# A hybrid decoder step: the 32x32 inverses of the delta net on one compact tile that ScalarE fills and empties

## Chip, cores and metric

The kernel runs on one core of a Trainium2 chip. The metric is the time of one execution on the device in microseconds (us), as the median of several runs. TensorE is called PE here, VectorE DVE, ScalarE ACT, GpSimd POOL, and SyncE, which issues the DMAs, SP.

## The reference

Two decoder layers run over a prompt of 512 tokens and 8 sequences of 8 new tokens, 576 tokens in all, of width 1024. Layer 0 has a pooling mixer, layer 1 a gated delta net, and each is followed by a SwiGLU FFN of width 2816. All is float32. The change is in the delta net, which the reference computes in chunks of 64 tokens (the kernel takes 128):

```python
kb = k * beta[..., None]
a_mat = jnp.where(strict, jnp.einsum('bhnid,bhnjd->bhnij', kb, k) * decay, 0.0)
t_mat = a_mat + jnp.eye(CHUNK, dtype=jnp.float32)
solve = functools.partial(lax.linalg.triangular_solve, left_side=True, lower=True, unit_diagonal=True)
u = solve(t_mat, v * beta[..., None])
w = solve(t_mat, kb * jnp.exp(gc)[..., None])
...
def step(S, inp):
    u_i, w_i, qk_i, qd_i, kd_i, gl_i = inp
    v_new = u_i - jnp.einsum('bhck,bhkv->bhcv', w_i, S)
    o_i = jnp.einsum('bhck,bhkv->bhcv', qd_i, S) + jnp.einsum('bhcs,bhsv->bhcv', qk_i, v_new)
    S = S * gl_i[..., None, None] + jnp.einsum('bhck,bhcv->bhkv', kd_i, v_new)
    return S, o_i
```

The unit triangular matrix of each head and chunk has to be inverted. 16 heads by 4 chunks of 128 tokens make 64 matrices of 128x128.

## The kernel before

**Work.** Large products are made of three passes with operands split into a high and a low part (`wh`, `wl` of the weights; `hH`, `hL` of the activations). `Weights.load` brings a weight block by DMA (`wraw`), ACT writes `wh`, and DVE or POOL subtracts to give `wl`. The stages follow each other: layer 0 with its FFN, the delta net in four groups G of four heads, its output projection, and the FFN of layer 1.

**A group.** `project(G)` computes q, k, v of the group (PSUM tile `ps_m`, two banks in turn; ACT moves them out to `u`, DVE convolves them in `ac`). `core(G)` is the delta rule: DVE writes the 16 triangular matrices of the group into `Uw` (128 partitions, 16 matrices, 128 columns), `inv32` inverts the four 32x32 diagonal blocks of all 16, and products on PE (`ps_k`, `ps_s`, with ACT between them in `Rs`, `T01`, `R2`) merge the blocks to 128x128. `braid` writes `inv32` down together with `sample_front`, the same step for the sample group, and `scan` with `sample_heads` follows.

**inv32.** `A` (tile `ia`) receives the transposed blocks, each column twice, and `X` (the first half of tile `ii`) begins as the identity `eye2`. For m from 31 down to 1, DVE multiplies into a scratch `tv` (the second half of `ii`) and subtracts from X: 62 small instructions. Before that, one DVE transpose for each of the four partition blocks reads `Uw` directly (`ia<-Uw`), and after it one for each writes back (`Uw<-ii`). The next user of the blocks is `T01` (`T<-Uw`, DVE), and then PE.

**Order.** Nothing is issued as it is written. All calls are recorded by `Plan`, with their dependences on tiles and banks, and `finish` places them on the five engines by ranks and costs (`forward`). Instructions that are marked EITHER go to DVE or POOL. Where a gap of PE in the plan is long, `idle_until` fills it with matmuls on an unused bank (`ps_w<-ones`). Last, `refined` goes through the program in windows and stirs the ranks by the seeds in the table `CHOSEN`, so another table gives another order everywhere. All recorded instructions therefore carry line 531, where they are issued, and the fillers line 527.

Of the kernel before, what the change touches and what calls it, by code (L numbers as in the profile page):

```python
# [14 lines left out]
AF = mybir.ActivationFunctionType  # L15
# [5 lines left out]
P = 128  # L21
# [35 lines left out]
class Plan:  # L57
# [755 lines left out]
def hybrid_kernel(  # L813
# [593 lines left out]
    def inv32(ap_, W):  # L1407
# [5 lines left out]
        for b in range(4):  # L1413
            s = slice(32 * b, 32 * b + 32)
            DVE.transpose(A[s], W[s, :, 32 * b:32 * b + 32].rearrange("p h i -> p i h").unsqueeze(2)
                          .to_broadcast([32, 32, 2, 16]))
            yield 1.2
# [817 lines left out]
```

## Time and profile before

| | |
|---|---|
| median of 3 runs | 1526.5 us (1526.38 to 1527.4) |
| the profiled execution's own time | 1525.06 us |
| its span, from the first to the last instruction | 1523.3 us |
| granted PE clock, mean | 0.997 |
| instructions | 30379 |

Rows of a group give: line, engine, operation, tile written and tiles read, shapes, count, then busy us in all, mean ns of one, and the engine's idle time before them with what ended it. Names of tiles leave buffer numbers out (`T` is `T01`). PEld is PE's loading of weights, which overlaps its matmuls. A float32 matmul shows as two records, so a filler counts twice in the trace and once in the order.

### The profile page before, as it was taken

The page shows a single profiled execution, that of the slowest core. Times are in us where ns is not written, and L with a number is a line of the kernel's source. Part 1 is how long each engine was busy: PE and PEld are TensorE (multiplying, and loading weights), DVE is VectorE, ACT ScalarE, POOL GpSimd, SP SyncE. Part 2 cuts the span into 40 slices and gives each one's busy share as a digit, 9 for nine tenths or more (in the row PEclk, how much of TensorE's full clock was granted, in tenths as well). Part 3 has the DMA queues.
Part 4 walks back from the last instruction along what each step waited for, and adds up shares of the span by engine and source line. Part 5 has one row for each costly group of instructions (what it writes and reads, how often), then busy time and mean ns, then how long its engine had stood idle before and what let it go on. Part 6 is the DMA issues. An engine that isn't in the chain of part 4 may idle for free.

```text
span 1523.3 us, 30379 instructions
## 1 busy us (share of the span) xinstructions
PE 1501.0 (99%) x11850; PEld 1452.8 (95%) x11850; DVE 1155.7 (76%) x2284; ACT 840.6 (55%) x1815; POOL 129.4 (8%) x269
## 2 busy tenths in 40 slices
PE   8999999999999999999999999999999999999997
PEld 7999999999999899899899899999999999999997
DVE  6993566678688698997899799667896476766865
ACT  7753543435466975764763764545565453534553
POOL 4210000000011010121120120100110000000000
PEclk9999999999999999999999999999999999999999
DMA  6563323233457433335433544657765333233263
GB/s 190 156 188 110 98 74 111 67 99 104 148 170 204 114 88 111 102 103 147 111 112 93 147 127 128 202 158 220 240 184 155 109 87 96 83 89 110 66 196 99
DMA packets 344902, 197.86 MB, mean 130 GB/s; under 512 B 13547, under 2 KB 337740, under 8 KB 344751
## 3 DMA queue, kind: packets, MB, share of 16 engines
q1 hardware_dynamic: 344759, 195.92, 44.6%
q8 instruction: 93, 1.52, 0.4%
q14 instruction: 50, 0.41, 0.1%
HBM read 165.60 MB, written 30.52 MB: 129 GB/s over the span
## 4 chain that ended last, share of the span: by engine, by line
PE 88%; DVE 6%; ACT 3%; DMA 2%; issue 1%; POOL 0%; SPq 0%; DVEq 0%; ACTq 0%; POOLq 0%
PE ps_B L531 29%; PE ps_A L531 26%; PE ps_m L531 19%; PE ps_s L531 5%; PE ps_k L531 5%; PE ps_x L531 2%; PE ps_e L531 1%; DVE wl L531 1%; PE ps_n L531 1%; DVE Uw L531 1%; DMA vt<-z_d 1%; DVE ac L531 1%; ACT wh L531 1%; DMA wraw<-in_gdn_w_in_dram 0%; DMA yo<-y_d 0%
## 5 line engine op out<-in xcount | busy, mean ns | idle before, releaser
L531 ACT ACTIVATE wh<-wraw 128x1024 fp32r<-128x1024 f32 (+4 forms) x239 | 232.5, 978 | 201.5 <-PE ps_B L531 79.6
L531 DVE TENSOR_TENSOR wl<-wraw,wh 128x1024 fp32r<-128x1024 f32 (+4 forms) x231 | 258.3, 1122 | 76.0 <-ACT wh L531 40.3
L531 PE MATMUL ps_m<-hH,wh 128*128 128x320 f32 (+1 forms) x832 | 251.5, 313 | 0.0
L531 PE MATMUL ps_m<-hL,wh 128*128 128x320 f32 (+1 forms) x832 | 247.5, 306 | 0.1
L531 PE MATMUL ps_m<-hH,wl 128*128 128x256 f32 (+1 forms) x832 | 245.8, 308 | 0.1
L531 PEld LDWEIGHTS ps_m<-hH,wh 128*128 128x128 f32 x832 | 155.1, 190 | 4.0 <-issue 1.0
L531 PEld LDWEIGHTS ps_m<-hL,wh 128*128 128x128 f32 x832 | 156.0, 190 | 2.0 <-issue 0.8
L531 PEld LDWEIGHTS ps_m<-hH,wl 128*128 128x128 f32 x832 | 154.7, 190 | 1.7 <-issue 0.4
L531 PE MATMUL ps_B<-hH,wh 128*128 128x320 f32 (+1 forms) x444 | 127.8, 304 | 0.2
L531 PE MATMUL ps_B<-hL,wh 128*128 128x320 f32 (+1 forms) x444 | 127.1, 304 | 0.0
L531 PE MATMUL ps_B<-hH,wl 128*128 128x320 f32 (+1 forms) x444 | 127.1, 304 | 0.0
L531 PE MATMUL ps_A<-hH,wh 128*128 128x256 f32 (+1 forms) x432 | 119.4, 292 | 0.0
L531 PE MATMUL ps_A<-hL,wh 128*128 128x256 f32 (+1 forms) x432 | 117.7, 290 | 0.0
L531 PE MATMUL ps_A<-hH,wl 128*128 128x256 f32 (+1 forms) x432 | 117.5, 291 | 0.1
L531 PE MATMUL ps_B<-aL,wh 128*128 128x288 f32 x352 | 100.0, 296 | 0.0
L531 PE MATMUL ps_B<-aH,wl 128*128 128x288 f32 x352 | 99.2, 297 | 0.7 <-DVE wl L531 0.7
L531 PE MATMUL ps_B<-aH,wh 128*128 128x288 f32 x352 | 99.1, 298 | 0.5 <-DVE xa L531 0.5
L531 PE MATMUL ps_A<-aL,wh 128*128 128x288 f32 x352 | 98.3, 296 | 0.0
L531 PE MATMUL ps_A<-aH,wl 128*128 128x288 f32 x352 | 97.7, 297 | 0.0
L531 PE MATMUL ps_A<-aH,wh 128*128 128x288 f32 x352 | 97.1, 297 | 0.0
L531 PEld LDWEIGHTS ps_B<-hH,wh 128*128 128x128 f32 x444 | 81.7, 188 | 0.7 <-ACT wh L531 0.6
L531 DVE SCALAR_TENSOR_TENSOR ac<-u,cwt,ac 128x600 f32<-128x600 f32 x96 | 79.5, 837 | 3.3 <-ACT ac L531 3.1
(463 smaller groups left out, 4040.8 us busy)
## 6 DMA issues: line engine op xcount, KB each, us to landing
wraw<-in_ffn_w_in_dram SPq DMA_DIRECT2D x77, 512.0 KB
wraw<-in_gdn_w_in_dram SPq DMA_DIRECT2D x56, 512.0 KB
graw<-in_ffn_w_in_dram SPq DMA_DIRECT2D x33, 512.0 KB
wraw<-in_ffn_w_out_dram SPq DMA_DIRECT2D x32, 448.0 KB
wraw<-in_gdn_w_out_dram SPq DMA_DIRECT2D x24, 512.0 KB
wraw<-in_ffn_w_out_dram SPq DMA_DIRECT2D x32, 320.0 KB
St<-in_state_gdn_rec_dram SPq DMA_DIRECT2D x32, 256.0 KB
out_dram<-St SPq DMA_DIRECT2D x32, 256.0 KB
```

The costliest lines, as they stand in the source:

```text
L531: calls[e](*a, **k)
```

## The change

`inv32` gathers the four diagonal blocks of `Uw` into the second half of `ii` with four ACT copies, each 32 partitions by 512. One DVE transpose over all 128 partitions then fills `A`. At the end one DVE transpose over 128 partitions writes the result into the second half of `ii`, and four ACT copies spread it back into `Uw`. The recursion between is untouched. The table `CHOSEN` is another one: 5 strings with 3206 numbers in the place of 6 with 3493. So the order of instructions differs through the whole program, and which of the EITHER instructions go to POOL too.

```diff
     CHOSEN = (
-        "0: 51633 4180 93590 78750 34477 23530 63076 77272 88530 16072 91213 50029 90818 92607 6488 48788 652 "
...
         A = ap_.tile([P, 32, 32], F32, name="ia", tag="ia", bufs=1)
         XT = ap_.tile([P, 2, 512], F32, name="ii", tag="ii", bufs=1)
         X = XT[:, 0].rearrange("p (j i) -> p j i", j=32)
+        D32 = XT[:, 1].rearrange("p (i h) -> p i h", h=16)
         for b in range(4):
             s = slice(32 * b, 32 * b + 32)
-            DVE.transpose(A[s], W[s, :, 32 * b:32 * b + 32].rearrange("p h i -> p i h").unsqueeze(2)
-                          .to_broadcast([32, 32, 2, 16]))
-            yield 1.2
+            ACT.activation(D32[s], W[s, :, s].rearrange("p h i -> p i h"), AF.Copy)
+        DVE.transpose(A, D32.unsqueeze(2).to_broadcast([P, 32, 2, 16]))
+        yield 1.2
         EITHER.tensor_copy(X, eye2)
...
+        DVE.transpose(XT[:, 1].rearrange("p (i j) -> p i j", j=32), X.rearrange("p j i -> p i j"))
         for b in range(4):
             s = slice(32 * b, 32 * b + 32)
-            DVE.transpose(W[s, :, 32 * b:32 * b + 32].rearrange("p h (i d) -> p i d h", d=2),
-                          X[s].rearrange("p j i -> p i j"))
+            ACT.activation(W[s, :, s].rearrange("p h i -> p i h"), D32[s], AF.Copy)
             yield 0.6
```

**The start of an inverse, third group (G = 2).** These are DVE's rows before, from the last matrices in `Uw` to the first step of the recursion; `des` belongs to the sample group and `ac` to the convolutions of the next group.

```order
1083 L531 SCALAR_TENSOR_TENSOR Uw<-ps_k,bet,QD 128x128 x2
1084 L531 RECIPROCAL oss<-oss 128x20
1085 L531 STREAM_TRANSPOSE ia<-Uw 32x1024 x4
1086 L531 TENSOR_TENSOR des<-des,s_st 128x128
1087 L531 TENSOR_TENSOR ii<-ia,ii 128x31
1088 L531 SCALAR_TENSOR_TENSOR ac<-u,cwt,ac 128x600
```

The same place on DVE in the changed kernel, where `BD` and `TQ` belong to the sample group:

```order
1071 L514 SCALAR_TENSOR_TENSOR Uw<-ps_k,bet,QD 128x128
1072 L514 TENSOR_TENSOR des<-des,s_in 128x128
1073 L514 TENSOR_TENSOR QD<-ps_k,QD 128x2x128 x2
1074 L514 TENSOR_TENSOR wl<-wraw,wh 128x1024
1075 L514 SCALAR_TENSOR_TENSOR BD<-ps_k,bet,des 64x64 x2
1076 L514 TENSOR_TENSOR TQ<-ps_k,des 64x64 x2
1077 L514 STREAM_TRANSPOSE ia<-ii 128x1024
1078 L514 SCALAR_TENSOR_TENSOR BD<-ps_k,bet,des 64x64
1079 L514 TENSOR_TENSOR ii<-ia,ii 128x31
```

And ACT there in the changed kernel, with the gather among the moves out of `ps_m`:

```order
728 L514 ACTIVATE QD<-QD,ngs 128x128
729 L514 ACTIVATE wh<-wraw 128x1024
730 L514 ACTIVATE ii<-Uw 32x512 x4
731 L514 ACTIVATE u<-ps_m 128x256
732 L514 ACTIVATE ks<-ps_k 128x128
733 L514 ACTIVATE u<-ps_m 128x8x8
```

One transpose stands in the place of four, a weight split and steps of the sample group moved ahead of it, and the four copies stand on ACT directly ahead of a move out of `ps_m`.

**The end of an inverse, first group (G = 0).** DVE before, from the last step of the recursion to the third transpose into `T01`:

```order
754 L531 TENSOR_TENSOR ii<-ii 128x16
755 L531 STREAM_TRANSPOSE Uw<-ii 32x32x16 x2
756 L531 STREAM_TRANSPOSE T_1431<-Uw 32x16x32 x2
757 L531 STREAM_TRANSPOSE Uw<-ii 32x32x16 x2
758 L531 SCALAR_TENSOR_TENSOR ac<-u,cwt,ac 128x600
759 L531 TENSOR_TENSOR wl<-wraw,wh 128x1024
```

DVE in the changed kernel:

```order
748 L514 TENSOR_TENSOR ii<-ii 128x16
749 L514 STREAM_TRANSPOSE ii<-ii 128x512
750 L514 TENSOR_TENSOR wl<-wraw,wh 128x1024
751 L514 STREAM_TRANSPOSE T_1431<-Uw 32x16x32 x2
752 L514 TENSOR_TENSOR wl<-wraw,wh 128x1024
753 L514 STREAM_TRANSPOSE T_1431<-Uw 32x16x32
```

ACT in the changed kernel, where `zz` is a gate projection that is moved out of `ps_m`:

```order
513 L514 ACTIVATE u<-ps_m 128x256
514 L514 ACTIVATE Uw<-ii 32x32x16 x4
515 L514 ACTIVATE wh<-wraw 128x1024
516 L514 ACTIVATE zz<-ps_m 128x256
517 L514 ACTIVATE Rs_1432<-ps_k 32x16x32 x2
```

The four transposes back became one transpose and four copies on ACT, and a weight split fills DVE's wait for the copies.

**PE at the start of the third group's inverse.** Before, with the fillers `ps_w` around the first products of the sample group (`qks`):

```order
4614 L531 MATMUL ps_s<-gts,s_gt_r 128x256
4615 L531 MATMUL ps_k<-qk 128x256
4616 L527 MATMUL ps_w<-ones 128x128
4617 L531 MATMUL ps_k<-qks 128x128
4618 L531 MATMUL ps_k<-ident,qks 128x128
4619 L527 MATMUL ps_w<-ones 128x128 x4
4620 L531 MATMUL ps_m<-hH,wh 128x256
```

In the changed kernel the first product of the sample group stands among projections, with no filler near:

```order
4647 L514 MATMUL ps_m<-hH,wh 128x320
4648 L514 MATMUL ps_m<-hL,wh 128x320
4649 L514 MATMUL ps_k<-qks 128x128
4650 L514 MATMUL ps_m<-hH,wl 128x320
4651 L514 MATMUL ps_m<-hH,wh 128x320
4652 L514 MATMUL ps_k<-ident,qks 128x128
```

Counted over the whole order, there are 42 fillers before and 36 now: 8 and 9 at the start, 6 and 6 at the change from layer 0 to layer 1, 18 and 9 in the four groups of the delta net, 10 and 12 at the end. The eight `wl` splits that POOL made before are on DVE now. ACT has 31 table loads where it had 30.

384 rows, old and new, of the table CHOSEN are left out of this document.

## The prediction

> **What bounds the kernel now.** I read the page first, then the table of stretches, the groups by form, and the chain of waits inside the delta net. The page's first part, busy time by engine, its DVE row by slices, and its chain:
>
> ```profile
> PE 1501.0 (99%) x11850; PEld 1452.8 (95%) x11850; DVE 1155.7 (76%) x2284; ACT 840.6 (55%) x1815; POOL 129.4 (8%) x269
> DVE  6993566678688698997899799667896476766865
> PE 88%; DVE 6%; ACT 3%; DMA 2%; issue 1%; POOL 0%; SPq 0%; DVEq 0%; ACTq 0%; POOLq 0%
> ```
>
> PE is the bound: it is idle for 1523.3 - 1501.0 = 22.3 us, and every matmul of the reference is still there after the change. What can change is how well PE is fed. The table of stretches tells where it isn't; after the stretch and its length come busy us of PE, PEld, DVE, ACT and POOL, then clock and DMA.
>
> ```profile
> 0.00:38.00 38.00, 32.34 (x219) 29.78 (x220) 25.08 (x72) 28.97 (x70) 17.81 (x77) 0.91 0.69 190
> 440.00:520.00 80.00, 78.30 (x629) 73.75 (x628) 65.42 (x136) 56.99 (x131) 8.08 (x17) 1.00 0.61 168
> 520.00:975.00 455.00, 449.96 (x3921) 420.10 (x3920) 400.46 (x963) 287.31 (x808) 75.29 (x144) 1.00 0.43 123
> 1100.00:1460.00 360.00, 359.94 (x2718) 359.02 (x2718) 252.39 (x408) 173.55 (x270) 5.10 (x6) 1.00 0.39 114
> 1460.00:1523.00 63.00, 53.69 (x402) 50.93 (x400) 36.53 (x63) 30.89 (x57) 0.00 (x0) 0.97 0.47 140
> ```
>
> The four groups of the delta net are 520 to 975 us. DVE is busy for 400.46 of 455 us there (88%), against 70% in the last FFN. PE shows 5.04 us of idle time, and PEld is busy for 92.3%, against 99.7% in the FFN. So DVE is nearly full where the change relieves it, but PE's own row leaves little to win. Start and end hold 5.66 and 9.31 us of idle PE, which this code doesn't touch.
>
> The Trainium skill, in "Perfetto Trace Analysis", Identifying the Most-Contended Engine, says that matmul busy time is a poor measure of headroom and that the busy share of weight loads is a good one. By it the stage would have 34.9 us to give where the matmul row has 5.04. The FFN's row agrees with the rule, but the stage also loads many narrow weights, so I take it as a ceiling.
>
> **The change part by part.** The groups by form, with busy us and mean ns of one:
>
> ```profile
> L531 DVE STREAM_TRANSPOSE ia<-Uw 32x1024 f32<-32x1024 f32 x16 | 32.6, 2034 | 0.2
> L531 DVE STREAM_TRANSPOSE Uw<-ii 32x512 f32<-32x512 f32 x16 | 18.2, 1138 | 0.4
> L531 DVE STREAM_TRANSPOSE T<-Uw 32x512 f32<-32x512 f32 x12 | 8.4, 701 | 0.3
> L531 ACT ACTIVATE s1h<-s1raw 128x512 fp32r<-128x512 f32 x33 | 20.8, 629 | 26.9 <-DVE s1raw L531 12.5 <-PE ps_A L531 8.0 <-PE ps_B L531 6.3
> L531 DVE COPY ii<-eye 128x512 f32<-128x512 f32 x3 | 1.3, 417 | 0.0
> L531 POOL TENSOR_TENSOR wl<-wraw,wh 128x1024 fp32r<-128x1024 f32 x8 | 19.3, 2414 | 18.5 <-ACT wh L531 18.5
> L531 DVE TENSOR_TENSOR wl<-wraw,wh 128x1024 fp32r<-128x1024 f32 x151 | 184.4, 1225 | 39.4 <-ACT wh L531 22.9 <-PE ps_B L531 7.8 <-PE ps_A L531 7.2
> L531 ACT ACTIVATE u<-ps_m 128x256 f32<-128x256 f32 x56 | 20.7, 375 | 19.1 <-PE ps_m L531 18.6 <-PE ps_x L531 0.3
> L531 ACT ACT_TABLE_LOAD x29 | 37.2, 1283 | 1.1 <-DMA misc<-in_gdn_a_log_dram 0.7
> L527 PE MATMUL ps_w<-ones 128*128 128x128 f32 x84 | 14.4, 300 | 1.3 <-POOL ones L306 1.3
> ```
>
> *DVE's load.* Removed: 32.6 + 18.2 = 50.8 us. Added: four transposes of 1024 and four of 512, now over 128 partitions. The trace has none over 128. A transposed element takes 701 / 512 = 1.37 ns where source and target run densely (`T<-Uw`), and 2.0 to 2.2 ns in the two removed forms. So the 1024 costs 1.40 to 2.03 us, and I take 1.40, since its source is dense now. The 512 costs 0.70 to 1.14 us, and I take 1.14, since its source still strides. Together that is 10.2 us (8.4 to 12.7), and DVE is relieved by 40.6 us. The eight splits that come over from POOL cost DVE 8 x 1.225 = 9.8 us of it. That leaves about 31 us, and DVE's share of the stage falls from 88% to 81%. On its own this is worth nothing in time, since PE is the bound.
>
> *ACT's load.* 32 copies of 512 at 0.629 us make 20.1 us. No ACT row of this size has a strided operand; strides make DVE's transposes 1.45 to 1.6 times as long, so the bounds are 20 to 32 us, and I take 20, as the copies read or write densely on one side. ACT has 455 - 287.31 = 167.7 us free in the stage, which hides it. One more table load is 1.28 us of ACT, hidden as well (0 to 1.3).
>
> The Trainium skill speaks against these copies: "ScalarE: Activation LUTs", Rules for kernel authors, wants simple elementwise work on VectorE and not on ScalarE. The one copy of 512 on DVE agrees, with 0.417 us against 0.629. By that rule the 32 copies would be 13.3 us on DVE and the relief 27 us in place of 40.6; with ACT's free time in the stage I follow the load and not the rule.
>
> *The end of an inverse.* The chain of waits inside the first group's end, then the fourth's (start us, us, what):
>
> ```profile
> 585.82 1.13 DVE Uw L531
> 586.98 1.17 DVE Uw L531
> 588.17 0.70 DVE T L531
> 588.88 0.70 DVE T L531
> 589.60 0.88 DVE Uw L531
> 590.78 1.14 DVE Uw L531
> ...
> 950.88 1.07 DVE Uw L531
> 951.99 1.16 DVE Uw L531
> ...
> 955.78 1.14 DVE Uw L531
> ```
>
> The transposes back lie on the chain in these two groups; in the second and third the chain runs elsewhere. From 585.82 to 591.92 they take 6.10 us. After the change, one transpose of 1.14, then four copies of 0.629 one behind the other, 3.66 us, with both `T` transposes on DVE beside the copies. So 2.4 us less in each of the two, 4.9 us on the chain. But DVE and PE wait on each other all along here, and PE is busy beside it: shortening the chain helps only where PE would else run dry. I can bound this from 0 to -4.9 us, and take the middle, -2.4.
>
> *The start of an inverse.* DVE is held for 8.09 us in one piece now (the timeline of DVE, then of ACT, in the third group):
>
> ```profile
> 779.64 8.09 DVE L531 STREAM_TRANSPOSE ia<-Uw 32x1024 f32<-32x1024 f32 x4
> 785.24 0.50 ACT L531 ACTIVATE u<-ps_m 128x256 f32<-128x256 f32 x2 [3.12 <-PE ps_m L531]
> ```
>
> After: four copies, 2.5 us, and 1.40 us of transpose, about 4 us shorter. None of these four pieces is on the chain, so I take 0 for the latency (bounds 0 to -4 us a group). The waits that it adds: the transpose waits for ACT's copies, and behind it stands the recursion; in the third group a split of 1.2 us and steps of the sample group stand ahead of it and cover half of the copies. If that cover is gone, the recursion starts up to 2.5 us later, still earlier than now. The copies also need `ii` free of the states that were stored from it, which only the identity copy needed so early before.
>
> *The fillers.* PE is given fillers where the plan leaves it a gap, so their count tells of gaps. 84 records in 14.4 us are 42 fillers of 0.34 us. The stage has 18 now and 9 after: -3.1 us. Start and end have 3 more: +1.0 us. Net -2.1 us (0, if the gaps are only left empty, to -3.1).
>
> *Sum.* 0 (loads) - 2.4 (ends of inverses) - 2.1 (gaps) = -4.5 us. Against the profiled execution, 1525.06 us (the span of 1523.3 and 1.8 around it), that is 1520.6. Its own time lies 1.4 us under the median of the runs, so on the median 1526.5 - 4.5 = 1522.0 us.
>
> **The rivals.** *No change.* PE shows no idle time that DVE could fill: 449.96 of 455 us. Then what leaves DVE's chain turns up as PE's own, fillers only hid gaps that other waits keep, and the time is 1526.5 to 1525, say 1525.5. For it: 88% of the chain is PE already. Against it: half the fillers of the stage are gone.
>
> *More than forecast.* If the weight loads' row is the true headroom, the end of every inverse counts in full: 4 x 2.4 + 2.1 = 11.7 us, 1514.8. For it: 92.3% against 99.7%. Against it: in two groups the chain passes elsewhere.
>
> *Slower: the copies hold up the moves out of `ps_m`.* ACT works in order, and at the eight places the four copies stand as a block of 2.5 us directly ahead of, or close to, `u<-ps_m` or `zz<-ps_m`. The projections have two banks. How fast PE fills one, from a long run of them in the chain:
>
> ```profile
> 780.72 12.80 PE ps_m L531 x96
> ```
>
> And a weight split's copy on ACT, from its timeline:
>
> ```profile
> 787.04 1.06 ACT L531 ACTIVATE wh<-wraw 128x1024 fp32r<-128x1024 f32 x1 [1.29 <-PE ps_m L531]
> ```
>
> 24 matmuls to a bank make 3.2 us. A move needs 0.375 us, so PE stops once a finished bank waits longer than 2.8 us for ACT. The block alone stays 0.3 us under that. With one such split of 1.06 us caught between, PE loses 0.76 us at each of the eight places, 6.1 us; with the fillers' gain that is 1530.5. It decides as soon as ACT reaches the block more than 0.3 us after a bank is finished. For it: in the order a split stands right ahead of the block in the third group. Against it: ACT waited 3.12 us for PE just there.
>
> A reordering of the rest can go either way by a few us; it widens each case and isn't one of its own.
>
> **How the numbers follow.** The forecast has 0.45, more than forecast 0.10, no change 0.22, slower 0.23. The predicted time is the forecast's, 1522.0 us; its own range is 1518.5 (both terms at their far ends, -8.0) to 1523.4. The whole range goes from 1516.5, into the larger gain, to 1530.0, into the slower case; about 0.16 is left out. A run of this kernel can be told from no change by about 0.2%, 3 us. So faster has 0.45 + 0.10 = 0.55, same 0.22, slower 0.23.
>
> **What would show it.** Right: transposes near 1.4 and 1.1 us, copies near 0.63; DVE near 370 us in the four groups; fewer `Uw` pieces of DVE on the chain; PE's idle time in the stage under 5 us; the stage some 4 us shorter, start and end within 1 us of now. Wrong: `ps_m` waiting for ACT's `u` or `zz` at the blocks (the slower rival); a stage of the same length with another releaser in front of PE (no change); a gain in the stages without an inverse, which would put the cause on the order and not on the copies.

## The result, and the profile after

| | before | after |
|---|---|---|
| median | 1526.8 us (1525.0 to 1529.2, 20 runs) | 1529.1 us (1526.9 to 1531.4, 20 runs) |
| the profiled execution's own time | 1525.06 us | 1530.0 us |
| its span | 1523.3 us | 1528.2 us |

The ratio is 1.0014, with a 95% interval of 1.0008 to 1.0021. The kernel became slower, by 2 us, where 4.5 us of gain were forecast. That is less than the 3 us that the prediction asked for to tell a run from no change, but the interval leaves out 1. The forecast's direction was wrong. The time lies near the rival "Slower: the copies hold up the moves out of `ps_m`", which had 1530.5 us.

First the page after, busy time by engine and the engines of its chain:

```profile
PE 1497.1 (98%) x11838; PEld 1448.7 (95%) x11838; DVE 1128.6 (74%) x2282; ACT 878.3 (57%) x1848; POOL 110.3 (7%) x247
PE 54%; ACT 4%; DVE 4%; DMA 3%; issue 1%; SPq 0%; DVEq 0%; ACTq 0%
```

PE is busy for 3.9 us less, and yet the span is 4.9 us longer (2.3 us in the medians, since the profiled execution was faster than its median before and slower than it after): PE's idle time went from 22.3 to 1528.2 - 1497.1 = 31.1 us. The table of stretches after says where (columns as before):

```profile
0.00:38.00 38.00, 31.56 (x220) 28.70 (x220) 24.79 (x71) 28.79 (x70) 16.68 (x76) 0.96 0.67 190
440.00:520.00 80.00, 79.44 (x640) 75.21 (x639) 64.25 (x138) 56.60 (x130) 11.47 (x20) 1.00 0.57 161
520.00:975.00 455.00, 440.14 (x3868) 411.44 (x3867) 375.52 (x960) 323.82 (x839) 54.01 (x121) 1.00 0.42 121
```

In the delta net PE is idle for 14.86 us in place of 5.04. DVE has 25 us less there, where 31 were forecast, and ACT 36.5 us more, where 20 were expected. The groups by form after give the reason:

```profile
L514 ACT ACTIVATE ii<-Uw 32x512 f32<-32x512 f32 x16 | 17.9, 1122 | 2.2 <-DVE Uw L514 2.1
L514 ACT ACTIVATE Uw<-ii 32x512 f32<-32x512 f32 x16 | 17.9, 1118 | 2.0 <-DVE ii L514 1.7
L514 DVE STREAM_TRANSPOSE ia<-ii 128x1024 f32<-128x1024 f32 x4 | 5.0, 1245 | 7.7 <-ACT ii L514 7.7
L514 DVE STREAM_TRANSPOSE ii<-ii 128x512 f32<-128x512 f32 x4 | 4.3, 1084 | 0.1
```

The timeline of ACT in the third group shows one gather:

```profile
780.43 1.06 ACT L514 ACTIVATE wh<-wraw 128x1024 fp32r<-128x1024 f32 x1 [0.42 <-PE ps_m L514]
781.39 4.47 ACT L514 ACTIVATE ii<-Uw 32x512 f32<-32x512 f32 x4
785.89 0.38 ACT L514 ACTIVATE u<-ps_m 128x256 f32<-128x256 f32 x1
```

A copy takes 1.12 us, not 0.63, so the four of them hold ACT for 4.5 us, not 2.5. The move of `u` out of its bank stands right behind. PE's timeline at that place:

```profile
784.53 0.39 PE L514 MATMUL ps_k<-ident,qks 128*128 128x128 f32 x2
786.32 0.39 PE L514 MATMUL ps_m<-hH,wh 128*128 128x256 f32 x1 [1.41 <-ACT u L514]
```

And what PE waits for in the four groups, five rows of its waits (releaser: us in all, times, longest):

```profile
PE ps_m L514 <- ACT u L514: 3.4, 3, 1.5
PE ps_x L514 <- DVE vt L514: 3.0, 4, 1.2
PE ps_k L514 <- ACT Uw L514: 2.0, 3, 0.8
PE ps_k L514 <- DVE TQ L514: 1.6, 2, 1.5
PE ps_x L514 <- ACT nco L514: 1.6, 1, 1.6
```

In the third group both banks were full, and PE stood for 1.41 us until ACT came back. Before, none of ACT's `u`, `Uw` or `zz` was among PE's releasers in this stretch. The three waits for `u` stand behind gathers; the fourth gather, in the first group, costs in another way: DVE's transpose waits for the copies, `TQ` stands behind it on DVE, and PE waits 1.5 us for `TQ`. The waits for `Uw` stand behind the copies back. The chain at the first group's end, which before ran through 6.10 us of DVE's transposes, now runs through ACT (start us, us, what):

```profile
582.08 1.10 DVE ii L514
...
584.38 1.12 ACT Uw L514
...
585.53 1.09 ACT Uw L514
...
586.64 1.07 ACT Uw L514
...
587.75 2.05 PE ps_k L514 x62
```

From 582.08 to 587.75 that is 5.67 us, against the 3.66 us forecast.

### The profile page after: what moved, and what is told of

It is laid out like the page before. It is cut to its first block, busy times and chain, and to the rows that moved or that the text cites. A ratio compares the mean times of both kernels' runs of the same rounds, so it can differ in the third digit from the quotient of the medians.

```text
span 1528.2 us, 30405 instructions
## 1 busy us (share of the span) xinstructions
PE 1497.1 (98%) x11838; PEld 1448.7 (95%) x11838; DVE 1128.6 (74%) x2282; ACT 878.3 (57%) x1848; POOL 110.3 (7%) x247
## 4 chain that ended last, share of the span: by engine, by line
PE 54%; ACT 4%; DVE 4%; DMA 3%; issue 1%; SPq 0%; DVEq 0%; ACTq 0%
PE ps_B L514 15%; PE ps_m L514 14%; PE ps_A L514 13%; PE ps_s L514 5%; PE ps_k L514 4%; PE ps_x L514 2%; ACT Uw L514 1%; DMA vt<-z_d 1%; ACT ii L514 1%; DVE ii L514 1%; DMA yo<-y_d 1%; PE ps_n L514 1%; DVE Uw L514 1%; DVE vt L514 0%; ACT L514 0%
## 5 line engine op out<-in xcount | busy, mean ns | idle before, releaser
L514 DVE TENSOR_TENSOR wl<-wraw,wh 128x1024 fp32r<-128x1024 f32 (+4 forms) x239 | 268.4, 1127 | 68.2 <-ACT wh L514 31.5
L514 PE MATMUL ps_m<-hH,wl 128*128 128x320 f32 (+1 forms) x832 | 244.4, 308 | 0.0
L514 PE MATMUL ps_A<-aH,wh 128*128 128x288 f32 x352 | 100.7, 297 | 0.0
L514 PEld LDWEIGHTS ps_B<-hH,wl 128*128 128x128 f32 x444 | 81.8, 188 | 0.6 <-DVE wl L514 0.5
L514 PEld LDWEIGHTS ps_B<-hL,wh 128*128 128x128 f32 x444 | 81.9, 188 | 0.1
```

The lines of the kernel that those rows point to most:

```text
L514: calls[e](*a, **k)
```

## The experiments

**How an operand is changed and nothing else.** Another operand would change the plan and with it the whole order. So in most experiments the plan is made with the old operands, and a helper `swap` then replaces those of the instruction recorded last. The order of all engines stays what it was. The kernel before was timed again beside each group of experiments, at 1526.1, 1525.7 and 1525.4 us where it had 1526.8 beside the changed kernel, so times of different groups are compared by their ratios to it.

### The copies made dense

After the change a copy reads or writes `D32`, where an element's neighbour along the row of a matrix is 16 elements (64 bytes) away. The tile is laid out here matrix by matrix, so that a copy moves runs of 32 elements, and the striding falls to the two transposes:

```diff
+        DH = XT[:, 1].rearrange("p (h i) -> p h i", h=16)
...
             ACT.activation(D32[s], W[s, :, s].rearrange("p h i -> p i h"), AF.Copy)
+            plan.swap(DH[s], W[s, :, s], AF.Copy)
         DVE.transpose(A, D32.unsqueeze(2).to_broadcast([P, 32, 2, 16]))
+        plan.swap(A, DH.rearrange("p h i -> p i h").unsqueeze(2).to_broadcast([P, 32, 2, 16]))
...
         DVE.transpose(XT[:, 1].rearrange("p (i j) -> p i j", j=32), X.rearrange("p j i -> p i j"))
+        plan.swap(DH.rearrange("p h (i d) -> p i d h", d=2), X.rearrange("p j i -> p i j"))
...
             ACT.activation(W[s, :, s].rearrange("p h i -> p i h"), D32[s], AF.Copy)
+            plan.swap(W[s, :, s], DH[s], AF.Copy)
```

> The changed kernel with every instruction on its engine in the same place; only the two access patterns of the compact tile are swapped: it is laid out matrix by matrix, so that the 32 copies on ScalarE run densely and the 8 transposes do the striding. Theory 1 (the copies are too long: 1.12 us each measured with a strided side, 0.63 us assumed, a block of four 4.5 us, and PE stands idle right behind seven of the eight blocks for 7.0 us in all): copies near 0.6 us, ScalarE about 16 us less busy, PE's idle time in the four groups from 14.9 us back to about 8, and the time 5 to 7 us under the changed kernel's 1529.1, so 1522 to 1524. Rival 2 (the new order is poorer by itself, whatever the copies cost): copies shorter, but the time stays at 1528 to 1530. Transposes of 1024 near 2.0 us instead of 1.25 under both.

Measured: 1518.5 us, ratio 0.9952 (0.9940 to 0.9965). Its groups by form, then its stretch:

```profile
L519 ACT ACTIVATE ii<-Uw 32x512 f32<-32x512 f32 x16 | 10.0, 627 | 2.3 <-DVE Uw L519 2.2
L519 ACT ACTIVATE Uw<-ii 32x512 f32<-32x512 f32 x16 | 10.1, 628 | 2.2 <-DVE ii L519 1.9
L519 DVE STREAM_TRANSPOSE ia<-ii 128x1024 f32<-128x1024 f32 x4 | 8.3, 2082 | 0.2 <-ACT ii L519 0.2
```

```profile
520.00:975.00 455.00, 447.89 (x3945) 418.25 (x3945) 382.99 (x968) 311.86 (x853) 51.72 (x121) 1.00 0.44 124
```

PE's wait for `u` in the four groups, and ACT's timeline in the third:

```profile
PE ps_m L519 <- ACT u L519: 0.2, 1, 0.2
```

```profile
776.67 2.54 ACT L519 ACTIVATE ii<-Uw 32x512 f32<-32x512 f32 x4
779.23 0.39 ACT L519 ACTIVATE u<-ps_m 128x256 f32<-128x256 f32 x1
```

Its chain at the first group's end:

```profile
580.01 4.66 PE ps_m L519 x35
584.67 1.99 PE ps_k L519 x64
```

The copies take the 0.63 us that the prediction took, the block is 2.5 us, and PE waits for `u` no more than 0.2 us. PE's idle time in the stretch is 7.1 us in place of 14.9, and the inverse has left the chain at its end. The same order is 9.5 us faster than the changed kernel by the ratios (10.6 in the medians), although its transposes are longer (2.08 and 1.17 us). This version beats both kernels.

### Only the gather dense, only the way back dense

Each takes half of the diff above; the compact tile has the other layout for the other half.

> As the dense kernel, but only at the start of each inverse: the gather copies run densely and the first transpose strides; the copies back stay strided. Same places on all engines. Theory 1: the waits of PE behind the gather (1.5, 1.4 and 0.5 us for a move out of ps_m, and 1.5 us for the sample group in the first inverse) go, the others stay: 3 to 4 us under 1529.1, so about 1525.5. Rival 2: 1528 to 1530.

> As the dense kernel, but only at the end of each inverse: the copies back run densely, the last transpose strides on both sides; the gather stays strided. Same places on all engines. Theory 1: the waits of PE for the blocks of Uw (0.4 + 0.8 and 0.8 us) and for the copy out of ps_x behind the block (1.6 us) go: 2 to 4 us under 1529.1, so about 1526. Rival 2: 1528 to 1530.

Measured: 1525.4 us (ratio 0.9995, 0.9986 to 1.0004) and 1525.1 us (0.9992, 0.9983 to 1.0001). PE's waits in the four groups, of the kernel with the dense gather and then of that with the dense way back:

```profile
PE ps_k L519 <- ACT Uw L519: 2.0, 3, 0.8
PE ps_m L519 <- ACT u L519: 0.2, 1, 0.2
```

```profile
PE ps_m L519 <- ACT u L519: 3.4, 3, 1.5
PE ps_k L519 <- DVE TQ L519: 1.5, 1, 1.5
```

Each half takes away the waits behind its own blocks and leaves the others: behind the gathers stand `u` and `TQ`, behind the copies back `Uw`. By the ratios the halves are worth 2.9 and 3.4 us, and both together 9.5. The 3 us between are about what the intervals allow, so it stays open whether the halves help each other.

### The relief of DVE alone, in the order of before

In the kernel before, the transposes at both ends were cut to one of full size and pieces of 32x32, so most of their work is left out. Their count and the order stay.

```diff
                           .to_broadcast([32, 32, 2, 16]))
+            if b == 0:
+                plan.swap(A.rearrange("p a b -> p (a b)"), W[:, :8].rearrange("p h i -> p (h i)"))
+            else:
+                plan.swap(A[s, 0], W[s, 0, s])
...
+            plan.swap(W[s, 0, s], XT[s, 0, :32])
```

> The kernel before, every instruction in its place, with most of the 32 transposes' work left out: of the four ahead of each inverse the first runs over 128x1024 densely and the others over 32x32, and each of the four behind it over 32x32. VectorE is relieved of about 42 us and nothing is added on ScalarE; the outputs are not the inverse's. It prices the relief alone in a fixed order. The prediction's reading (the ends of two inverses lie on the chain, the starts are worth nothing): 0 to 5 us under 1526.8. If PE is bound by its own work all along: no change. If VectorE's long block is what starves PE: 6 us or more under.

Measured: 1525.0 us, ratio 0.9993 (0.9984 to 1.0002). Its stretch:

```profile
520.00:975.00 455.00, 450.02 (x3926) 420.34 (x3925) 366.81 (x964) 287.44 (x808) 79.79 (x144) 1.00 0.43 123
```

DVE has 34 us less and PE exactly what it had, 450.02 against 449.96 us. In that order the relief alone is worth about 1 us, and by its interval anything from 2.4 us to nothing. The chain at the first group's end, which ran through DVE's transposes in the kernel before, now runs through PE's own work:

```profile
589.07 3.10 PE ps_m L536 x20
592.17 2.01 PE ps_k L536 x64
```

So the end of the inverse is shorter there, and PE's own matmuls take its place on the chain.

### The other loop order of the copies

Perhaps the distance of 512 bytes in `Uw` was what cost. Here the loops of a copy are exchanged, so that it runs along 32 elements of `Uw` and the single elements, 64 bytes apart, are on the compact side. Layout and order are those of the changed kernel.

```diff
-            ACT.activation(D32[s], W[s, :, s].rearrange("p h i -> p i h"), AF.Copy)
+            ACT.activation(D32[s].rearrange("p i h -> p h i"), W[s, :, s], AF.Copy)
...
-            ACT.activation(W[s, :, s].rearrange("p h i -> p i h"), D32[s], AF.Copy)
+            ACT.activation(W[s, :, s], D32[s].rearrange("p i h -> p h i"), AF.Copy)
```

> The changed kernel with only the loop order inside the 32 copies exchanged: on the side of the big tile they now take runs of 32 neighbours (512 bytes from run to run), and on the side of the compact tile single elements 64 bytes apart; its layout, the transposes and every place in the order stay. If any single-element stride costs ScalarE 1.12 us: copies 1.1 us, time 1528 to 1530. If only the far stride of 512 bytes does: copies 0.63 us, transposes 1.25 us, PE's waits behind the blocks gone, 1516.5 to 1518.5, as fast as the dense kernel's 1518.5 or a little faster, since the transpose ahead of each inverse is 0.8 us shorter.

Measured: 1528.3 us, ratio 1.0014 (1.0005 to 1.0023). The copies:

```profile
L514 ACT ACTIVATE ii<-Uw 32x512 f32<-32x512 f32 x16 | 17.6, 1099 | 1.6 <-DVE Uw L514 1.5
L514 ACT ACTIVATE Uw<-ii 32x512 f32<-32x512 f32 x16 | 17.6, 1099 | 1.4 <-DVE ii L514 1.1
```

A step of 64 bytes costs nearly as much as one of 512, on the side that is read and on the side that is written.

### Blocks of other lengths

If the length of a block on ACT is what costs, dense copies must cost too once there are more of them. In the dense kernel's order one, two or three copies of each block are issued twice (blocks of 3.1, 3.8 and 4.4 us); in another kernel one copy is of 128 partitions and the other three are cut to 32x32 (1.3 us), so most of the data isn't copied.

```diff
+            plan.twice(2 if b < 3 else 1)
```

> The dense kernel (1518.5) with its blocks of copies shortened further, each instruction in its place: of four copies the first runs over 128x512 and the three others over 32x32, so a block takes about 1.3 us in place of 2.5; most of the data is left uncopied, and the outputs are not the inverse's. If there is a point below which a block costs nothing, as the slower rival of the prediction has it (a block under about 2.8 us): 1517.5 to 1519. If the time goes with the length of the blocks (10.6 us for 2.0 us a block between the changed and the dense kernel): 6 us less, near 1512.5.

> The dense kernel, same order, with one of the four copies of each block issued twice: a block of 5 x 0.628 = 3.1 us. By the threshold of 2.8 us at most 0.3 us is lost at each of eight places: 1518.5 to 1521 us. If the price came from the strides as such and not from the block's length: 1518.5.

> As with five copies, now six: a block of 3.8 us, 1.0 us over the threshold, at most 8 us at eight places. Where the copies stand right ahead of a move about half of it shows: 1521 to 1526 us. If the strides as such were the price: 1518.5 to 1519.5.

> As before with seven copies: a block of 4.4 us, as long as that of the changed kernel (4.5), but of dense copies. If the block's length is what costs: about 1529 us, the changed kernel's time, with PE waiting for u, zz and Uw behind the blocks. If the strides cost in another way (the traffic of the memory, say): 1518.5 to 1521.

Measured:

| block on ACT | time | ratio to before | PE idle, profiled execution |
|---|---|---|---|
| 1.3 us | 1519.1 us | 0.9958 (0.9945 to 0.9970) | 22.3 us |
| 2.5 us (the dense kernel) | 1518.5 us | 0.9952 (0.9940 to 0.9965) | 21.2 us |
| 3.1 us | 1523.3 us | 0.9986 (0.9976 to 0.9995) | 24.3 us |
| 3.8 us | 1528.3 us | 1.0019 (1.0010 to 1.0029) | 27.3 us |
| 4.4 us | 1535.9 us | 1.0069 (1.0052 to 1.0086) | 31.1 us |
| 4.5 us (the changed kernel, strided) | 1529.1 us | 1.0014 (1.0008 to 1.0021) | 31.1 us |

With seven copies, the groups of the gather, the stretch, and PE's waits in it:

```profile
L524 ACT ACTIVATE ii<-Uw 32x512 f32<-32x512 f32 x28 | 17.6, 628 | 2.7 <-DVE Uw L524 2.2
```

```profile
520.00:975.00 455.00, 438.99 (x3827) 409.64 (x3828) 376.14 (x955) 319.12 (x855) 52.73 (x121) 0.99 0.42 118
```

```profile
PE ps_m L524 <- ACT u L524: 3.8, 4, 1.5
PE ps_k L524 <- DVE TQ L524: 3.1, 2, 2.3
PE ps_k L524 <- ACT Uw L524: 2.2, 4, 1.0
```

A block of 1.3 us gains nothing over one of 2.5; above that each copy more in every block costs 5 to 8 us. With five, six and seven copies the time is over the upper end of what was expected each time, by 2 to 7 us. By the rival's 2.8 us the block of 3.1 could have cost 0.3 us at eight places, 2.4 us; it cost 4.8. In its four groups PE waits 0.6 us for `u` and 0.7 for `zz`, but also 1.3 us for `TQ` (0.4 in the dense kernel), which waits for the gather by way of DVE. So the cost begins between 2.5 and 3.1 us, near the 2.8 that the rival had worked out, but the banks of `ps_m` aren't all of it.

The waits of the changed kernel come back with copies that are all dense, and PE's idle time is the same 31.1 us: the length of the block costs, not the strides as such.

With seven copies the kernel is nevertheless 8 us slower than the changed one by the ratios (6.8 in the medians, 4.2 in the profiled spans). The 4.2 us are PE's busy time, 1501.3 against 1497.1 us for the same 11838 records, and the granted clock shows where: in the four groups it falls to 0.50 at 554 to 556 and 592 to 594 us, shortly behind a wait of 2.33 us for `TQ` and two close waits of 1.02 and 0.35 us for `Uw`. In the changed kernel, whose longest wait there is 1.60 us, it stays at 1.00. The wait for `TQ` is 0.86 us longer than in the changed kernel, and the strided transpose ahead of it takes 2.06 us for 1.25. That these waits bring the clock down is read from the order of events; no run varies it alone.

Two more tests of the block are not made: no run sets the moves out of `ps_m` between the copies, and none puts the copies on DVE, which the prediction considered.

### DVE's work put back into the new order

The dense kernel with each of its eight transposes issued four times, which gives DVE the 39 us back.

```diff
+        plan.twice(4)
```

> The dense kernel of 1518.5 us, in the same order, with each of its eight transposes issued four times: DVE gets 4 x 3 x 2.08 + 4 x 3 x 1.17 = 39 us back, so the start of an inverse holds DVE for 8.3 us and its end for 4.7 us, as before the change (8.1 and 4.6). If the gain of 8 us over the kernel before is DVE's relief, it goes: about 1526 us. If the gain lies in the order, which only needed the shorter work to be planned, it stays: 1518 to 1520 us.

Measured: 1569.7 us, ratio 1.0285 (1.0266 to 1.0305), far over both expectations. Its stretch, then DVE's timeline and PE's in the first group:

```profile
520.00:975.00 455.00, 420.06 (x3453) 393.18 (x3452) 388.31 (x928) 282.93 (x783) 48.42 (x118) 0.95 0.37 104
```

```profile
546.88 8.06 DVE L524 STREAM_TRANSPOSE ia<-ii 128x1024 f32<-128x1024 f32 x4
...
556.86 0.23 DVE L524 TENSOR_TENSOR TQ<-ps_k,des 64x64 f32<-64x64 f32 x1
```

```profile
557.23 0.66 PE L524 MATMUL ps_k<-ident,BD 128*128 128x128 f32 x2 [6.38 <-DVE TQ L524]
```

The order puts steps of the sample group behind the transpose, since it counts on a short one. With 8.06 us there, `TQ` comes 6 us late, and PE stands for 6.38 us. PE is idle for 34.9 us in the stretch, 28 us more than in the dense kernel, and the granted clock is 0.95 in it. Over the whole execution PE is idle for 33 us more than in the dense kernel and busy for 17 us more, with the same number of matmuls, at a mean clock of 0.979 for 0.995. So the relief is needed by the new order, though the old order couldn't use it.

### The tables exchanged

Is the gain then the order's, whatever the work? Before's code with the changed kernel's table, and the changed code (with the loops exchanged) with before's table:

> The kernel before with the table of the changed kernel, which was not made for it: nothing but the order differs from before. It prices what a table is worth that was made for the code. If the order alone carries the dense kernel's gain of 7.6 us over before: 1520 or under. If a foreign table costs: 1530 to 1545.

> The kernel with the exchanged loop order and the table of before, which was not made for it. Together with the run before this one it tells what the change's relief of VectorE is worth when neither code has a table of its own: both plans are drawn without a fit. If the relief is worth some 5 to 10 us to the planner: 5 to 10 us under the kernel before with the new table. If the dense kernel's gain is its table's fit: equal to it within some 4 us. ScalarE's copies 0.63 or 1.12 us as in the first run of these four; at 1.12, 10 us more.

Measured: 1598.0 us (ratio 1.0469, 1.0452 to 1.0486) and 1581.6 us (1.0370, 1.0352 to 1.0388). A table under a code for which it wasn't found costs 53 to 72 us, far more than the change; the first was expected at 1530 to 1545 us. The changed code fares 16 us better under a foreign table, strided copies included, which fits the relief; but each plan comes out so differently that this pair settles nothing.

## Why the prediction was wrong

**The step that failed: ACT's load.** It took 0.629 us for a copy "as the copies read or write densely on one side", with bounds of 20 to 32 us for all. Measured were 1.12 us and 35.8 us, outside the bounds. The upper bound came from DVE's strided transposes, which are 1.45 to 1.6 times as long as dense ones; on ACT the strided copy is 1.79 times as long (1.122 / 0.627). A single strided side is enough for it, and runs of 32 elements are as fast as fully dense rows (0.627 against 0.629 us).

The Trainium skill, "SBUF — State Buffer", Door 1: The DMA port swizzle, says in a note that SBUF works in lines of 16 bytes and that an access pays each time it goes to a new line. The trace agrees in kind: both steps are longer than a line, and both cost nearly the same (1.10 us at 64 bytes, 1.12 us at 512). The prediction didn't weigh that rule, and the Trainium skill gives no price for it there.

**The slower rival.** Its place was right, and so was one of its waits. PE waits for `u` behind three of the four gathers, 3.4 us, and for `zz` not at all, where 6.1 us at eight moves were worked out. The larger part of the 9.8 us that PE's idle time in the stretch grew by is in waits that the rival didn't name: 2.0 us for the blocks of `Uw` behind the copies back, `TQ` behind the first gather, and steps such as `nco`. That its 1530.5 us came so near to 1529.1 is in part luck. It was refused since the block of 2.5 us stayed 0.3 us under the 2.8 us at which PE would stop; with the true price the block was 4.5 us, 1.7 over. Its counter-argument, that ACT waited 3.12 us for PE just there, went with the old order: in the changed kernel ACT waits 0.42 us ahead of that block. The upper end of the term's own bounds, 32 us, would have made the block 4.0 us and turned the rival into the forecast: the bound was kept for the sum, where ACT's free time hides it, and not carried into the rival, where it decides.

**The end of an inverse.** Forecast were 3.66 us for it, -2.4 us in time. With the changed kernel it was 5.67 us. With the price that was assumed, in the dense kernel, the end isn't on the chain at all. No run shows the -2.4 us as a gain: in the order of before, a shorter end (and start) only put PE's own work on the chain, and in the dense kernel PE waits more in the stretch than before, 7.11 us for 5.04.

**The start of an inverse.** The transpose took 1.245 us for 1.40, the one back 1.08 for 1.14. The start was taken at no cost; the 4.5 us that ACT is held there is the first half of the loss. DVE's transposes wait 7.7 us for the four gathers (the row `ia<-ii`), and with them what stands behind on DVE.

**The fillers.** The forecast had six fewer, 12 records:

```profile
L510 PE MATMUL ps_w<-ones 128*128 128x128 f32 x72 | 11.3, 302 | 1.3 <-POOL ones L289 1.3
```

They are 3.1 us less busy PE (14.4 before), and PE's whole busy time fell by 3.9 us. This didn't become time, since the waits behind the blocks took more.

**DVE's load.** That it was worth nothing on its own held in the order of before (1 us, at most 2.4, with 34 us less on DVE) for the reason given, PE's row. It didn't hold as a statement on the change: under the new order the same work, put back, costs 51 us. The relief is worth what the order makes of it.

**The sum.** Where the copies cost what was assumed, the profiled span is 1518.7 us, 4.6 us under before, against 4.5 in the forecast; 3.5 of it is less work on PE and 1.1 less waiting. The medians are 7.6 us apart. The direction was right at that price, and the one price turned it round. That 4.6 meets 4.5 is luck. The fillers gave 3.1 for 2.1 us. PE waits less outside the stretch of the inverses, by 1.0 us at the start (0 to 38 us), 1.3 at the change of layers (440 to 520) and 1.2 at the end (from 1460), and 2.1 us more inside it. The prediction itself had named gains in the stages without an inverse as the sign that the cause lies in the order. Its own range also stopped at 1523.4, though the near ends of its two terms, 0 and 0, give 1526.5. How much of the dense kernel's gain is the order's and how much the relief's can't be split further: neither works without the other.

**The headroom.** By the Trainium skill's rule on weight loads ("Perfetto Trace Analysis", Identifying the Most-Contended Engine) the stretch had 34.9 us to give. In the dense kernel PEld is busy for 418.25 us there, 1.9 us less than before, while the kernel is faster; no run here shows that headroom used.

## What to carry to other kernels

Price an instruction by its access pattern and not by its element count alone: a copy whose single elements lie apart on one side took 1.8 times as long on ACT. When work is moved to an engine with much free time, its total doesn't tell the cost; compare the longest block that it forms with the time that the buffers behind it cover (here 2.5 us cost nothing, and 3.1 us cost 5 us over eight places). Carry the upper bound of each duration into every rival that has a point of decision, and put the strides on the engine where nothing waits right behind.

## What the runs showed of the hardware

- ACT, 32x512 float32: 0.627 us in runs of 32 elements, 1.10 us with single elements 64 bytes apart on one side, 1.12 us with 512 bytes, reading or writing alike.
- DVE's transpose of 1024 elements a partition took 2.08 us over 128 partitions and 2.03 us over 32, both from strided sources, so one instruction over 128 did the work of four. From a dense source it took 1.245 us.
- The granted clock, as a mean over the stretch of 455 us, was 1.00 with up to 14.9 us of idle PE, 0.99 with 16.0 us (seven copies) and 19.1 us (the kernel before under the changed kernel's table), 0.97 with 20.2 us (the changed code under before's table) and 0.95 with 34.9 us (DVE's work put back). Within it the clock was 0.50 for 2 us or more from the end of a wait of 6.38 us (DVE's work put back, 556 to 560 us) and shortly behind one of 2.33 us (seven copies, 554 to 556 us), and 1.00 throughout the stretch in the changed kernel, whose longest wait there was 1.60 us. How long a wait has to be isn't measured.
